# Where buffers live in a two-layer decoder step: normed tokens, partial sums and token-major weights moved to other slots

## The chip, the cores and the metric

The kernel runs on one core of one Trainium2 chip. The metric is the device time of one launch in microseconds (us). The kernel before the change takes 1732.09 us, the median of three runs that lie between 1731.93 and 1732.36 us.

## The reference: what is computed

One inference step of a two-layer decoder runs for a prompt of 512 tokens and for 8 samples of 4 new tokens each. Both groups share the weights, so the kernel treats them as one block of 544 tokens of width 1024. All of it is in float32. Layer 0 has one input projection that feeds a state-space branch and a sliding-window attention, and one output projection. Layer 1 has forgetting attention over a paged cache. Each layer then attends to 256 memory tokens, and ends with a feed-forward part:

```
h = rms_norm(x, norm_ffn[l])
g, u = split(h @ w_ffn_in[l])        # 1024 -> 2 x 2816
x = x + (silu(g) * u) @ w_ffn_out[l]
```

Outputs are the two normed token blocks, the new states and the new cache rows.

## The kernel before, in words

**Operands in two halves.** A float32 product is made of three TensorE products of rounded halves. Whatever TensorE reads, weights and tokens alike, is split first: ScalarE (ACT) writes the rounded high part, VectorE (DVE) subtracts it from the source and writes the low part. `wpiece` (L141) does this for most weights: it loads a piece into `raw` (two buffers), and the halves go to `wh` and `wl` (three buffers each). A buffer taken from such a ring waits until the readers of its last content are done. Names in a profile row are tiles: `xh`, `xl` are halves of the tokens, `fh`, `fl` (and `f1`) those of the feed-forward weights, `ps` is a PSUM bank.

**Slots.** Large activations share 13 slots `H` of 128 x 2176 floats (L119). The two halves of the 544 tokens of a norm take four of these, the hidden values of the feed-forward part `hh` and `hl` one each per four tiles.

**The token-major weights.** In layer 0 the weights `we_v` (L601) multiply with tokens on the output partitions and give V and the state-space time steps; in layer 1 `wd_v` does the same (L973). Each is two pieces of 128 x 1088, loaded by `wpiece`, between the keys (`kT`, L428) and the queries (`we_q`).

**The feed-forward part** (`ffn`, L1469) makes 22 hidden tiles of 128. The first three are plain (`plain`): per tile a gate and a value product for two token chunks, 256 and 288 wide, each followed by L1496 (gate times the norm's scale, DVE), L1497 (silu, ACT), L1498 (times the scale, POOL) and L1499 (value times gate, DVE), and by a split into `hh` and `hl` (L222, L225). The other 19 tiles use seven block products instead of eight: the weight's and the tokens' quarters are combined first. `factors` (L1436) loads a tile's weights (`fr`, two buffers, 1024 KB) and makes the sums s1 to s4 with DVE (L1457 to L1460) and all splits (L1450, L1451). `operands` (L1405) writes the normed tokens `xn`, makes the sums t1 to t4 with POOL (L1424, L1429), and splits them into seven factors `xf` (b11, b21, b22, t1 to t4; L1415 on ACT, L1417 or L1419 on DVE). Both `xn` (two) and `xf` (seven) are slots `H`. `product` (L1467) is 12 matmuls of 128 x 272.

Per tile the order is: `begin` (a11 x b11, copied to the partial sum S0 by L1540), `second` (a12 x b21, plus S0, L1546), `third` (s1 x t1; s2 x t2, copied to S1 by L1553), `fourth` of the tile before (s3 x t3, copied to S2 by L1557, summed to G1 by L1558, silu L1559), `last` (a22 x t4, silu L1564; s4 x b22, plus S1, L1567; gate times value L1569 on POOL; split). S0, S1, S2, G1 and the gate SG are parts of one tile `ft`, beside two value buffers U that alternate between tiles.

**What sets the order.** Each engine runs its instructions in program order. Neither that order nor the addresses stand in the source: a scheduler in the compiler orders the instructions by its own cost estimates, and a packer lays buffers that are not alive together over each other. A change of buffers therefore moves instructions and waits too. Loads are issued by SyncE (SP), also in order.

## Time and profile before

The profiled execution took 1733.22 us by the device clock; the span of its trace is 1731.4 us, so 1.8 us lie outside the span. Its mean granted TensorE clock is 0.983.

| | busy us | share of the span |
|---|---|---|
| PE (matmul) | 1666.6 | 96% |
| PEld (weight load) | 1531.3 | 88% |
| DVE | 1200.5 | 69% |
| ACT | 776.9 | 45% |
| POOL | 429.4 | 25% |

A row of a timeline reads: start in us, duration, engine, line, operation, output<-input, count, and in brackets the time for which the engine stood idle before it and what ended that. In a table of waits the numbers are the total, how many times, and the longest. In a table of stretches an engine's column is its busy time, with the count of its instructions, followed by the granted clock (PEclk, 1.00 is full speed), the share of the DMA engines, and GB/s.

### The profile page before, as it was taken

What the parts mean: (1) busy time and instruction counts of PE and PEld (TensorE: products, weight loads), DVE (VectorE), ACT (ScalarE), POOL (GpSimd) and SP (SyncE); (2) the same over time, 40 slices, a digit from 0 to 9 for tenths busy, and PEclk for the clock granted to TensorE, in tenths of its full rate; (3) what the DMA queues carried; (4) which work ended last, traced back from release to release, by engine and by line L of the source; (5) the groups of instructions that cost most, each with busy time, mean ns of one, the idle gap of its engine ahead of it and who ended that gap; (6) DMA issues with size and microseconds to landing.
All of it is one profiled execution on the core that took longest, in us unless ns stands there. A gap on an engine that the chain in (4) does not pass through costs nothing.

```text
span 1731.4 us, 32174 instructions
## 1 busy us (share of the span) xinstructions
PE 1666.6 (96%) x12824; PEld 1531.3 (88%) x12824; DVE 1200.5 (69%) x2142; ACT 776.9 (45%) x1575; POOL 429.4 (25%) x550
## 2 busy tenths in 40 slices
PE   6999999989999989999999999889999899999997
PEld 6988899866997989999999997556898899999997
DVE  6667679867866897777766567335577887777753
ACT  4345435344545454444435345325446354444443
POOL 5022323566422511111113013012222501111112
PEclk9999999989999999999999999899999999999999
DMA  4211423127533142222214423444442142323212
GB/s 157 90 50 50 131 93 129 44 94 253 182 98 135 62 146 86 97 98 86 98 40 135 149 62 113 159 171 151 166 143 91 65 148 92 107 78 110 86 47 80
DMA packets 57106, 189.24 MB, mean 109 GB/s; under 512 B 6044, under 2 KB 16060, under 8 KB 49084
## 3 DMA queue, kind: packets, MB, share of 16 engines
q1 hardware_dynamic: 55268, 184.83, 31.9%
q8 instruction: 101, 1.65, 0.4%
q10 hardware_dynamic: 1608, 1.83, 0.4%
q0 software_dynamic: 80, 0.52, 0.1%
q14 instruction: 49, 0.40, 0.1%
HBM read 172.22 MB, written 14.95 MB: 108 GB/s over the span
## 4 chain that ended last, share of the span: by engine, by line
PE 84%; DVE 7%; DMA 3%; ACT 2%; issue 1%; POOL 1%; SPq 1%; DVEq 0%; ACTq 0%; POOLq 0%
PE ps L135 59%; PE ps L1467 23%; PE ps L138 3%; DMA kv<-fox_kv 1%; DVE wl L152 1%; DMA raw<-we_x 1%; DVE fl L1451 1%; DVE xn L1409 1%; DVE xl L228 1%; SPq L1158 0%; DMA raw<-wfo 0%; POOL ft L1498 0%; DMA hb<-state 0%; DVE fr L1457 0%; DVE xs L853 0%
## 5 line engine op out<-in xcount | busy, mean ns | idle before, releaser
L1467 PE MATMUL ps<-xf,fh 128*128 128x272 f32 x1824 | 355.3, 291 | 11.4 <-DVE ft L1496 3.7
L135 PE MATMUL ps<-xh,wh 128*128 128x288 f32 (+1 forms) x1088 | 319.3, 295 | 8.8 <-ACT wh L151 7.9
L135 PE MATMUL ps<-xl,wh 128*128 128x288 f32 (+1 forms) x1088 | 319.5, 295 | 1.2 <-DVE xl L228 1.0
L135 PE MATMUL ps<-xh,wl 128*128 128x288 f32 (+1 forms) x1088 | 317.9, 293 | 1.9 <-DVE wl L152 1.9
L1467 PEld LDWEIGHTS ps<-xf,fh 128*128 128x128 f32 x1824 | 290.1, 190 | 13.6 <-ACT xf L1415 6.8
L1467 PE MATMUL ps<-xf,fl 128*128 128x272 f32 x912 | 258.2, 292 | 0.0
L135 PEld LDWEIGHTS ps<-xh,wh 128*128 128x128 f32 x1088 | 206.4, 190 | 12.6 <-ACT wh L151 7.9
L135 PEld LDWEIGHTS ps<-xl,wh 128*128 128x128 f32 x1088 | 206.3, 190 | 7.1 <-issue 4.9
L1569 POOL TENSOR_TENSOR ft<-ft 128x544 f32<-128x544 f32 x38 | 78.9, 2076 | 527.7 <-DVE ft L1567 512.7
L135 PEld LDWEIGHTS ps<-xh,wl 128*128 128x128 f32 x1088 | 206.5, 190 | 3.3 <-DVE wl L152 2.2
L151 ACT CAST wh<-raw 128x1024 fp32r<-128x1024 f32 (+2 forms) x128 | 130.9, 1023 | 173.8 <-PE ps L135 98.8
L1451 DVE TENSOR_TENSOR fl<-fr,fh 128x1024 fp32r<-128x1024 f32 x114 | 173.7, 1525 | 23.8 <-ACT fh L1450 23.6
L152 DVE TENSOR_TENSOR wl<-raw,wh 128x1024 fp32r<-128x1024 f32 (+2 forms) x128 | 160.7, 1256 | 30.4 <-ACT wh L151 15.2
L1467 PEld LDWEIGHTS ps<-xf,fl 128*128 128x128 f32 x912 | 170.8, 190 | 0.0
L1450 ACT CAST fh<-fr 128x1024 fp32r<-128x1024 f32 x114 | 119.8, 1053 | 94.0 <-DVE fr L1458 51.8
L135 PE MATMUL ps<-hl,oh 128*128 128x256 f32 (+1 forms) x512 | 147.4, 289 | 0.0
L135 PE MATMUL ps<-hh,ol 128*128 128x256 f32 (+1 forms) x512 | 147.1, 288 | 0.0
L135 PE MATMUL ps<-hh,oh 128*128 128x256 f32 (+1 forms) x512 | 146.2, 288 | 0.0
L237 POOL TENSOR_TENSOR room<-room,sq 128x256 f32<-128x256 f32 (+1 forms) x96 | 84.9, 886 | 184.7 <-ACT sq L236 182.7
L135 PEld LDWEIGHTS ps<-hl,oh 128*128 128x128 f32 x512 | 96.5, 188 | 0.0
L135 PEld LDWEIGHTS ps<-hh,oh 128*128 128x128 f32 x512 | 96.3, 189 | 0.0
L135 PEld LDWEIGHTS ps<-hh,ol 128*128 128x128 f32 x512 | 96.3, 188 | 0.0
(425 smaller groups left out, 3783.6 us busy)
## 6 DMA issues: line engine op xcount, KB each, us to landing
fr<-wfi SPq DMA_DIRECT2D x38, 1024.0 KB
or<-wfo SPq DMA_DIRECT2D x32, 512.0 KB
kv<-fox_kv SPq DMA_DIRECT2D x64, 256.0 KB
raw<-wo_e SPq DMA_DIRECT2D x16, 512.0 KB
xk<-mem_k SPq DMA_DIRECT2D x8, 1024.0 KB
xv<-mem_v SPq DMA_DIRECT2D x8, 1024.0 KB
raw<-we_x SPq DMA_DIRECT2D x12, 512.0 KB
raw<-wfi SPq DMA_DIRECT2D x12, 512.0 KB
```

The source lines that it names most:

```text
L135: self.nc.tensor.matmul(out, lhsT, rhs, start=start, stop=stop)
L138: self.nc.tensor.transpose(out, in_, self.ident[0:k, 0:k])
L151: nc.scalar.copy(hi[:, 0:n], raw[:, 0:n])
L152: nc.vector.tensor_tensor(lo[:, 0:n], raw[:, 0:n], hi[:, 0:n].bitcast(F32), ALU.subtract)
L228: return nc.vector.scalar_tensor_tensor(ll, src, g, hh.bitcast(F32), ALU.mult, ALU.subtract)
L237: nc.gpsimd.tensor_tensor(acc, acc, sq[:, 0:N], ALU.add)
L1409: nc.vector.scalar_tensor_tensor(xn[k], self.x[k], self.par[:, st["g"] + k:st["g"] + k + 1], st["b"], ALU.mult, ALU.mult)
L1450: nc.scalar.copy(hi, t)
L1451: nc.vector.tensor_tensor(lo, t, hi.bitcast(F32), ALU.subtract)
L1467: self.nc.tensor.matmul(ps, w[a][:, k], x[:, b, k], start=start and k == 0 and i == 0, stop=k == 3 and i == 2, skip_group_check=True)
L1569: nc.gpsimd.tensor_tensor(p["u"], p["u"], SG, ALU.mult)
```

## The change

- `we_v` and `wd_v` no longer use the ring of `wpiece`. The new `vpieces` takes three slots `H` (`vr`, `vh`, `vl`), and puts the two pieces side by side in each. The ring's tiles shrink from 1088 to 1024 columns.
- The normed tokens `xn` of the feed-forward part leave the slots `H` and get two buffers in the pool of that part.
- The partial sums S0, S1, S2 and G1 lose their buffers. S0 and S1 are written to the two halves of the value buffer U and summed in place; S2 and G1 are written into the gate's buffer, of which there are now two (G) that alternate between tiles.
- Two small buffers move: the QS tile loses 64 columns, and `ncs` of the paged attention moves into a tile that exists already.

No arithmetic is added or removed, and each engine has as many instructions as before.

```diff
@@ wpiece
-        raw = self.wp.tile([P, 1088], F32, tag="raw", bufs=2, name=self.nm("raw"))
+        raw = self.wp.tile([P, 1024], F32, tag="raw", bufs=2, name=self.nm("raw"))
...
+    def vpieces(self, src):
+        nc = self.nc
+        raw, hi, lo = self.H("vr"), self.H("vh", F32R), self.H("vl", F32R)
+        out = []
+        for i in range(2):
+            s = slice(1088 * i, 1088 * i + 1088)
+            nc.sync.dma_start(raw[:, s], src[i])
+            nc.scalar.copy(hi[:, s], raw[:, s])
+            nc.vector.tensor_tensor(lo[:, s], raw[:, s], hi[:, s].bitcast(F32), ALU.subtract)
+            out.append([t[:, s].rearrange("p (k w) -> p k w", w=272) for t in (hi, lo)])
+        return out
...
-            wv = [self.wpiece(I["we_v"][i], 4, 272) for i in range(2)]
+            wv = self.vpieces(I["we_v"])
...
-            wv = [self.wpiece(I["wd_v"][i], 4, 272) for i in range(2)]
+            wv = self.vpieces(I["wd_v"])
@@ operands
         xn = Big(self, "xn")
+        xn.h = [fp.tile([P, 4 * NT], F32, tag="xn", bufs=2, name=self.nm("xn")).rearrange("p (k t) -> p k t", k=4) for _ in range(2)]
@@ ffn
-            t = fp.tile([P, 10 * HT], F32, name="ft")
-            part = lambda a, n: t[:, HT * a:HT * (a + n)]
-            U, SG, S0, S1, S2, G1 = (part(0, 2), part(2, 2)), part(4, 2), part(6, 1), part(7, 1), part(8, 1), part(9, 1)
+            t = fp.tile([P, 4 * NT], F32, name="ft")
+            U, G = ([t[:, NT * i:NT * i + NT] for i in r] for r in ((0, 1), (2, 3)))
...
-                    g, s = U[n % 2][:, o:o + N], SG[:, o:o + N]
+                    g, s = U[n % 2][:, o:o + N], G[n % 2][:, o:o + N]
...
-                nc.scalar.copy(S0, R)
-                return {"n": n, "w": w, "R": R, "u": U[n % 2]}
+                nc.scalar.copy(U[n % 2][:, 0:HT], R)
+                return {"n": n, "w": w, "R": R, "u": U[n % 2], "g": G[n % 2]}
...
-                nc.vector.tensor_tensor(p["u"][:, 0:HT], R3, S0, ALU.add)
+                nc.vector.tensor_tensor(p["u"][:, 0:HT], R3, p["u"][:, 0:HT], ALU.add)
...
-                nc.scalar.copy(S1, p["R"])
+                nc.scalar.copy(p["u"][:, HT:NT], p["R"])
...
-                nc.scalar.copy(S2, p["R"])
-                nc.vector.tensor_tensor(G1, p["R2"], S2, ALU.add)
-                nc.scalar.activation(SG[:, HT:NT], G1, AF.Silu, scale=-1.0)
+                g = p["g"][:, HT:NT]
+                nc.scalar.copy(g, p["R"])
+                nc.vector.tensor_tensor(g, p["R2"], g, ALU.add)
+                nc.scalar.activation(g, g, AF.Silu, scale=-1.0)
...
-                nc.scalar.activation(SG[:, 0:HT], p["R"], AF.Silu, scale=-1.0)
+                nc.scalar.activation(p["g"][:, 0:HT], p["R"], AF.Silu, scale=-1.0)
...
-                self.last = nc.vector.tensor_tensor(p["u"][:, HT:NT], p["R2"], S1, ALU.add)
+                self.last = nc.vector.tensor_tensor(p["u"][:, HT:NT], p["R2"], p["u"][:, HT:NT], ALU.add)
```

The change moves lines as well: after it, the lines from L145 to L163 read the same up to L152, and those of the feed-forward part are 13 to 15 higher (L1415 becomes L1430, L1419 L1434, L1451 L1466, L1467 L1482, L1496 L1510, L1553 L1567). Tile numbers are 3 to 6 lower.

What the compiler makes of it, at three places:

DVE in layer 0, around the keys. `wl_40`, `wl_43` (after: `vl_40`) are low halves of `we_v`, the other `wl` those of the first `we_q` pieces; L279 (after: L292) copies the scale that the keys need. Before:

```order
L152 TENSOR_TENSOR wl_40_319<-raw_38_316,wh_39_318 128x1088
L271 TENSOR_SCALAR col_2_79<-ps_22_161 128x2
L152 TENSOR_TENSOR wl_43_325<-raw_41_322,wh_42_324 128x1088
L279 COPY room_70<-ps_23_166 128x256
L152 TENSOR_TENSOR wl_57_508<-raw_55_505,wh_56_507 128x1024
L428 TENSOR_TENSOR kT_206<-ps_34_212,room_70 128x256
L428 TENSOR_TENSOR kT_206<-ps_36_264,room_70 128x256
```

and in the changed kernel:

```order
L165 TENSOR_TENSOR vl_40_318<-vr_38_316,vh_39_317 128x1088
L284 TENSOR_SCALAR col_2_79<-ps_22_161 128x2
L165 TENSOR_TENSOR vl_40_318<-vr_38_316,vh_39_317 128x1088
L152 TENSOR_TENSOR wl_54_505<-raw_52_502,wh_53_504 128x1024
L152 TENSOR_TENSOR wl_60_564<-raw_58_561,wh_59_563 128x1024
L292 COPY room_70<-ps_23_166 128x256
L441 TENSOR_TENSOR kT_206<-ps_34_212,room_70 128x256
L441 TENSOR_TENSOR kT_206<-ps_36_264,room_70 128x256
```

Two `we_q` splits now stand ahead of the scale's copy, and none between it and `kT`. The loads of the two pieces wait for the two `we_k` splits, where they waited for the two `we_v` splits.

DVE in layer 0, where the seven-product part begins. `fl` are low halves of the weight sums, `xf` with L1419 or L1417 (after: L1434, L1432) those of t1 to t4 in this order. Before:

```order
L1460 TENSOR_TENSOR fr_1082_7165<-fr_1082_7165 128x512
L1451 TENSOR_TENSOR fl_1087_7177<-fr_1082_7165,fh_1086_7176 128x1024
L1451 TENSOR_TENSOR fl_1089_7182<-fr_1082_7165,fh_1088_7181 128x1024
L1496 TENSOR_TENSOR ft_6755<-ps_1080_7109,room_70 128x288
L1499 TENSOR_TENSOR ft_6755<-ps_1079_7054,ft_6755 128x256
L1419 TENSOR_TENSOR xf_1068_7027<-xn_1063_7006,xf_1068_7027 128x1088
L1417 SCALAR_TENSOR_TENSOR xf_1069_7031<-xn_1063_7006,xf_1069_7031 128x1088
L225 TENSOR_TENSOR hl_1042_6757<-ft_6755,hh_1041_6756 128x256
L1499 TENSOR_TENSOR ft_6755<-ps_1081_7110,ft_6755 128x288
L1419 TENSOR_TENSOR xf_1070_7034<-xn_1064_7011,xf_1070_7034 128x1088
L1419 TENSOR_TENSOR xf_1071_7038<-xn_1064_7011,xf_1071_7038 128x1088
```

and in the changed kernel:

```order
L1475 TENSOR_TENSOR fr_1079_7162<-fr_1079_7162 128x512
L1434 TENSOR_TENSOR xf_1065_7024<-xn_1060_7003,xf_1065_7024 128x1088
L1466 TENSOR_TENSOR fl_1084_7174<-fr_1079_7162,fh_1083_7173 128x1024
L1466 TENSOR_TENSOR fl_1086_7179<-fr_1079_7162,fh_1085_7178 128x1024
L1510 TENSOR_TENSOR ft_6752<-ps_1077_7106,room_70 128x288
L1432 SCALAR_TENSOR_TENSOR xf_1066_7028<-xn_1060_7003,xf_1066_7028 128x1088
L1513 TENSOR_TENSOR ft_6752<-ps_1076_7051,ft_6752 128x256
L1434 TENSOR_TENSOR xf_1067_7031<-xn_1061_7004,xf_1067_7031 128x1088
L1434 TENSOR_TENSOR xf_1068_7035<-xn_1061_7004,xf_1068_7035 128x1088
L238 TENSOR_TENSOR hl_1039_6754<-ft_6752,hh_1038_6753 128x256
L1513 TENSOR_TENSOR ft_6752<-ps_1078_7107,ft_6752 128x288
```

t1 moves ahead of both weight splits, t3 and t4 ahead of a value split. On ACT the high half of t1 moves ahead of both weight casts. The packer lays the next tile's weights (`fr_1090`) over `xn_1060`, so the load of these waits for t2 (`xf_1066`); before, it waited for `fl_1089`, the second weight split.

PE at the same place. After the 24 matmuls of s1 x t1 and s2 x t2, the program before went on with s3 x t3 (`xf_1070`, 12 matmuls), and then to four matmuls of the next tile (`fh_1094`). In the changed kernel the next tile's four (`fh_1091`) come first:

```order
L1482 MATMUL ps_1087_7182<-xf_1066_7028,fl_1084_7174 128x272
L1482 MATMUL ps_1098_7256<-xf_1062_7013,fh_1091_7238 128x272 x2
L1482 MATMUL ps_1099_7285<-xf_1063_7016,fh_1091_7238 128x272 x2
L1482 MATMUL ps_1087_7182<-xf_1067_7031,fh_1085_7178 128x272 x2
L1482 MATMUL ps_1087_7182<-xf_1067_7031,fl_1086_7179 128x272
```

On ACT the cast that gives `fh_1091` likewise moves ahead of the copy of S1 (L1567), on which s3 x t3 waits, because both use one PSUM bank. The order in layer 1 is the same. Elsewhere the scheduler also reorders the end of layer 0's mixing part (state-space output and the `wo_e` weights) and the last group of the paged attention (cache loads ahead of `wo_d` loads).

23 lines of the change are left out of this document (12 added, 11 removed).

## The prediction, made before the changed kernel was run

> **What bounds the kernel now.** I read the page's busy times first, then the table of PE's waits:
>
> ```profile
> PE 1666.6 (96%) x12824; PEld 1531.3 (88%) x12824; DVE 1200.5 (69%) x2142; ACT 776.9 (45%) x1575; POOL 429.4 (25%) x550
> ```
>
> ```profile
> PE ps L1467 <- DVE ft L1496: 3.7, 1, 3.7
> PE ps L1467 <- DVE xf L1419: 3.0, 2, 2.2
> PE ps L1467 <- ACT xf L1415: 2.6, 1, 2.6
> PE ps L1467 <- ACT ft L1553: 2.0, 4, 0.5
> PE ps L135 <- DVE kT L428: 1.8, 1, 1.8
> ```
>
> TensorE bounds the whole; the change touches no matmul, so it can move only PE's waits, the 64.8 us of the span in which PE is not busy. The waits quoted are those at its places: 10.3 us in the two starts of the seven-product part (3.7 + 3.0 + 2.6, and two of the four waits of 0.5) and 1.8 us at the keys. What a wait there costs besides is in the clock:
>
> ```profile
> 604.00:626.00 22.00, 16.74 (x107) 15.86 (x106) 20.36 (x24) 13.08 (x21) 5.32 (x3) 0.84 0.45 168
> 1364.00:1392.00 28.00, 22.92 (x162) 22.01 (x161) 27.07 (x25) 12.41 (x19) 14.72 (x7) 0.88 0.32 122
> 1000.00:1030.00 30.00, 29.09 (x235) 28.25 (x233) 21.22 (x46) 14.73 (x32) 2.86 (x8) 1.00 0.24 71
> ```
>
> The first two stretches are the starts, in layers 0 and 1; the third is undisturbed. In the starts DVE is busy 20.36 of 22 and 27.07 of 28 us: there DVE, not PE, is what lasts.
>
> **The keys (layer 0).** The chain of waits, then DVE:
>
> ```profile
> 24.56 4.14 DMA raw<-we_q
> 29.86 1.22 DVE wl L152
> ```
>
> ```profile
> 8.94 1.63 DVE L152 TENSOR_TENSOR wl<-raw,wh 128x1024 fp32r<-128x1024 f32 x1
> 23.26 1.28 DVE L152 TENSOR_TENSOR wl<-raw,wh 128x1088 fp32r<-128x1088 f32 x1
> 28.03 0.42 DVE L279 COPY room<-ps 128x256 f32<-128x256 f32 x1 [2.22 <-PE ps L135]
> 31.57 0.36 PE L135 MATMUL ps<-wh,xh 128*128 128x272 f32 x1 [1.79 <-DVE kT L428]
> ```
>
> The first `we_q` load leaves at 24.56, when the first `we_v` split frees its buffer; its split (29.86 to 31.08) is in front of `kT` on DVE. In the change the load waits for the first `we_k` split instead, which ends at 8.94 + 1.63 = 10.57, so the data are there some ten us earlier. Two splits of 1.22 us then fall into DVE's idle 2.22 us before the copy at 28.03, and overrun it by 0.2 us. `kT` follows the copy, at about 28.7 instead of 31.0, and PE's next work, which is ready at 31.57 - 1.79 = 29.78, need not wait: **-1.8 us**, bounds -1.8 and -1.0 (casts late by 0.8). No later wait of PE hangs on a load that this leaves where it was, so I let the gain reach the end. `wd_v` in layer 1 has the same cure but no wait of PE in the list: 0.
>
> **The start of the seven-product part, layer 0.** DVE, ACT, SP and PE of before:
>
> ```profile
> 608.55 0.68 DVE L1460 TENSOR_TENSOR fr<-fr 128x512 f32<-128x512 f32 x1
> 609.41 2.89 DVE L1451 TENSOR_TENSOR fl<-fr,fh 128x1024 fp32r<-128x1024 f32 x2 [0.19 <-ACT fh L1450]
> 612.23 0.45 DVE L1496 TENSOR_TENSOR ft<-ps,room 128x288 f32<-128x288 f32 x1
> 612.93 1.28 DVE L1419 TENSOR_TENSOR xf<-xn,xf 128x1088 fp32r<-128x1088 f32 x1
> 614.13 1.89 DVE L1417 SCALAR_TENSOR_TENSOR xf<-xn,xf 128x1088 fp32r<-128x1088 f32 x1
> 616.64 2.48 DVE L1419 TENSOR_TENSOR xf<-xn,xf 128x1088 fp32r<-128x1088 f32 x2
> ```
>
> ```profile
> 616.75 0.43 ACT L222 CAST hh<-ft 128x288 fp32r<-128x288 f32 x1 [1.02 <-DVE ft L1499]
> 619.82 0.39 ACT L1553 COPY ft<-ps 128x272 f32<-128x272 f32 x1 [2.64 <-PE ps L1467]
> 620.10 1.05 ACT L1450 CAST fh<-fr 128x1024 fp32r<-128x1024 f32 x1
> 621.05 0.62 ACT L1450 CAST f<-fr 128x512 fp32r<-128x512 f32 x1
> ```
>
> ```profile
> 612.33 0.33 SPq L1440 DMA_DIRECT2D fr<-wfi  x1
> ```
>
> ```profile
> 611.69 0.39 PE L1467 MATMUL ps<-xf,fh 128*128 128x272 f32 x1 [2.61 <-ACT xf L1415]
> 614.26 0.59 PE L1467 MATMUL ps<-xf,fh 128*128 128x272 f32 x1 [2.17 <-DVE xf L1419]
> 619.41 0.38 PE L1467 MATMUL ps<-xf,fl 128*128 128x272 f32 x1
> 620.26 0.52 PE L1467 MATMUL ps<-xf,fh 128*128 128x272 f32 x2 [0.47 <-ACT ft L1553]
> 622.51 1.78 PE L1467 MATMUL ps<-xf,f 128*128 128x272 f32 x12
> ```
>
> From 614.26 to 619.41 lie 22 matmuls, 0.23 us each; 12 from 620.26 to 621.87 take 0.13 each. So after 5 us of waiting PE is at about half rate for 5 us, 2.2 us lost beside the waits. The mark to hold on to: at 622.5 PE has done 40 matmuls (s1 x t1, s2 x t2, s3 x t3, four of the next tile).
>
> Now the new order with these durations. Until the last weight sum (L1460 ends 609.23) nothing moves. DVE then: t1 to 610.4 (1.2); the two weight splits to 613.1 (2.7); gate 613.5 (0.4); t2 to 614.8 or 615.4 (1.3 to 1.9); value 615.2; t3 and t4 to about 618. PE has t1 and the first split at 611.9 and does s1 x t1 until 613.2 to 614.2. s2 x t2 needs the copy of S0, which on ACT stands behind the gate's silu (after 613.5) and a value's high half (after 615.2): 616.0. It runs 616.0 to 618.7 at 0.23. So t1 and t2 are no longer late, and PE is ahead by 0.7 us here. But next come four matmuls of the next tile. Its load leaves after t2 at 614.8 instead of 612.33. How long it takes is in the DMA rates of that place, slices of 0.75 us from 600:
>
> ```profile
> GB/s 0 0 0 0 0 0 0 22 0 0 0 0 0 0 0 0 0 120 55 360 415 442 393 426 464 393 431 388 344 273 339 49 0 0 0 0 0 0 0 0
> ```
>
> The rate rises at 612.75, and 1024 KB are through by 616.5: 4.2 us from issue. So now 619.0; the cast stands behind a value's high half (L1499 ends 618.9, cast 0.43): 619.4 to 620.4. Then the four matmuls; the copy of S1 waits behind this cast and the next (0.62): 621.4; s3 x t3 runs from there, 12 matmuls, to 622.9 at 0.13 or 624.1 at 0.23. The 40 are done at 622.9 to 624.1 instead of 622.5: +0.4 to +1.6, **+1.0 us**. The earlier operands gain nothing, since the load that xn now holds up, and the queue behind it on ACT, take the place of the old wait. What follows (next tile's low half, 1.2 us after its cast; a22 x t4) is ready in time.
>
> The Trainium skill ("TensorE: Matmul & The Clock Gate", Part 1: The HAM clock gate) says that the clock halves after an idle window of about 3.4 us, and is released after about as long of work. Before, the trace agrees (4.8 us of waits, then half rate for 5 us). By that rule the new order, whose longest single wait here is 2.8 us, would stay at full clock, and the lower end, +0.4, would hold.
>
> **Layer 1** has the same order, another time:
>
> ```profile
> 1381.78 0.45 DVE L1496 TENSOR_TENSOR ft<-ps,room 128x288 f32<-128x288 f32 x1
> 1382.37 0.57 PE L1467 MATMUL ps<-xf,fh 128*128 128x272 f32 x1 [3.73 <-DVE ft L1496]
> 1383.81 0.59 PE L1467 MATMUL ps<-xf,fh 128*128 128x272 f32 x1 [0.87 <-DVE xf L1419]
> 1389.12 0.52 PE L1467 MATMUL ps<-xf,fh 128*128 128x272 f32 x2 [0.47 <-ACT ft L1553]
> ```
>
> Here s1 x t1 waits for the gate (L1496), since it needs that PSUM bank. t1 (1.3 us) moves ahead of it, so it ends 1.0 to 1.3 us later, at 1383.2; s1 x t1 runs to 1386.0, and the copy of S0 (behind a value) comes at 1386.2. s2 x t2 ends at 1388.1. The next tile's load leaves after t2 (1.9 us as in layer 0), at 1385.0, lands at 1389.2, is cast at 1390.3; S1 is copied at 1391.3, and s3 x t3 ends at 1392.8. Before, the 40 were done at 1389.12 + 2.2 (the same stretch as 620.26 to 622.51) = 1391.4: **+1.4 us**, from 0 to +3.
>
> **Partial sums in place.** In the steady tiles the copy of S0 now waits for the value buffer, so for the low half of the hidden values two tiles earlier:
>
> ```profile
> 666.57 0.71 DVE L225 TENSOR_TENSOR hl<-ft,hh 128x544 fp32r<-128x544 f32 x1
> 669.41 0.39 ACT L1540 COPY ft<-ps 128x272 f32<-128x272 f32 x1
> ```
>
> That split ends 2.1 us before the copy starts: 0. The third and fourth of the 0.5 us waits for S1 stand at the end of each layer, in an order that stays: 0.
>
> **The two other reordered places.**
>
> ```profile
> 410.00:458.00 48.00, 47.52 (x325) 42.68 (x324) 38.89 (x73) 23.25 (x45) 25.51 (x23) 0.96 0.66 228
> 1147.00:1222.00 75.00, 65.48 (x550) 40.56 (x549) 35.70 (x104) 33.94 (x96) 11.65 (x19) 0.98 0.58 203
> ```
>
> At the end of layer 0's mixing PE idles 0.5 us and loses 0.04 x 48 = 1.9 us of clock, so at most 2.4 us can be won; as much can be lost where work that filled a wait moves. I take 0, bounds -2.4 and +2.4. In the paged attention 9.5 us are idle, and the weights that come later (issued after the cache's loads) are used tens of matmuls later; fill work moves from one wait to another: 0, bounds -2 and +2.
>
> **The sum.** -1.8 + 1.0 + 1.4 = +0.6 us, on the profiled 1733.22 (1731.4 span and 1.8 around it), which is 1.1 above the median. Against the median: 1732.09 + 0.6 = **1732.7 us**.
>
> **Rivals.**
> - *The starts do gain.* For it: 10.3 us of waits there and 2.2 + 1.6 us of half clock (in layer 1, 22 matmuls from 1383.81 to 1388.4, 0.07 to 0.08 more than 0.13 each), 14.1 in all, and two of the operands really come earlier. Against it: DVE is full, and t4, whose end closes the DVE work, moves by 1 us only. If the next tile's load lands in 2 us less and the clock stays up, half of the 14.1 goes: -7.0 - 1.8 = -8.8, **1723.3**.
> - *The next tile's load becomes the bound.* Mechanism: issued after t2 and used ahead of s3 x t3, each us by which it lands later than 4.2 us after issue is a us of PE in both layers. Five loads are issued in that stretch; it decides from 5 us on. With 2.5 us more per layer: +0.6 + 5.0, **1737.7**. Against it: it is the first of the five.
> - *The sums in place bind*: if the low half is over 2.1 us later than now, each further 0.2 us costs 38 x 0.2 = 7.6 us: **1740.3**. Nothing in those tiles delays it.
> - *The early weights do not come early* (other loads in front, DVE's splits late): the 1.8 us stay, **1734.5**; that is inside "no change".
>
> **How the numbers follow.** A measurement of this kernel can tell about 0.2%, 3.5 us, from no change: 1728.6 to 1735.6. My forecast with its bounds (and the fourth rival) 55%, the gain 22%, the late load 20%, the sums 3%. Of the forecast's own range, 1729 to 1736.5, a little passes 1735.6; some of the late load's stays below it. So faster 0.23, same 0.54, slower 0.23. For 8 in 10 the range reaches halfway to the two larger rivals: 1727 to 1738.
>
> **What would show it.** Right: PE's wait at `kT` gone; in both starts the load `fr` issued behind L1432, PE waiting on the `fh` cast (L1465) where it waited for `xf`, the 40 matmuls done within 2 us of the old mark. Wrong: no wait for that cast and a clock of 1.00 in the starts (the gain); new waits of S0's copy in the steady tiles; the mixing's or the paged attention's stretch longer or shorter by over 2.5 us, which would make the sum one of places that I set to 0.

## The result, and the profile after

The changed kernel takes 1743.63 us (median of four runs, 1742.01 to 1744.77), beside 1732.01 us for the kernel before in the same comparison. The ratio is 1.0068 with a 95% interval of 1.0051 to 1.0085: 0.7% slower, outside the forecast's range. The profiled execution took 1743.81 us; its span is 1742.0, 10.6 us longer than before.

The page's busy times of the changed kernel, then PE's waits (total, times, longest):

```profile
PE 1670.2 (96%) x12824; PEld 1536.1 (88%) x12824; DVE 1198.0 (69%) x2142; ACT 767.9 (44%) x1575; POOL 432.8 (25%) x550
```

```profile
PE ps L1482 <- ACT fh L1465: 4.8, 3, 2.3
PE ps L1482 <- ACT xf L1430: 4.7, 1, 4.7
...
PE ps L138 <- DMA lg<-fox_logf,pg: 2.4, 1, 2.4
PE ps L135 <- DVE CmYi L964: 1.9, 1, 1.9
...
PE ps L1482 <- ACT ft L1554: 1.5, 1, 1.5
PE ps L1482 <- DVE fl L1466: 1.3, 1, 1.3
...
PE ps L135 <- POOL room L412: 1.2, 1, 1.2
```

The wait for `kT` is gone, and of the 3.0 us for t1 to t4 by DVE 0.6 us are left. In their place stand the cast of the next tile's weights (L1465), a wait for `xf` by ACT, a wait for a gather (`lg`), one for `CmYi` (state-space output), and one for POOL at the keys. PE is also 3.6 us longer busy with the same 12824 matmuls: part of the loss is clock.

**Where the time went.** Every kernel here has 12824 matmuls, so I cut each trace at the starts of the same matmuls by number, at places where the program orders agree. Each stage is the time between two such starts. The difference to the stage of before, in us (one profiled execution each):

| stage (matmul numbers; length before) | forecast | measured |
|---|---|---|
| start with keys (0 to 210; 37.7) | -1.8 | -1.15 |
| end of layer 0's mixing (2690 to 3200; 92.2) | 0 | **+5.75** |
| seven-product start, layer 0 (4130 to 4530; 59.7) | +1.0 | +2.26 |
| layer 1's first part with the gather (7200 to 7400; 27.4) | 0 | **+5.30** |
| paged attention (7700 to 9000; 200.3) | 0 | -3.08 |
| seven-product start, layer 1 (10100 to 10600; 71.1) | +1.4 | +2.57 |
| the six other stages together | 0 | -0.7 |

The sum of the measured column is +10.9; work behind the last of these starts gives 0.3 back. Two places that the forecast set to 0 make as much as the whole result.

### The profile page after: what moved, and what is told of

It reads as the page before. It is cut to its first block, busy times and chain, and to the rows that moved or that the text cites. A ratio compares the mean times of both kernels' runs of the same rounds, so it can differ in the third digit from the quotient of the medians.

```text
span 1742.0 us, 32009 instructions
## 1 busy us (share of the span) xinstructions
PE 1670.2 (96%) x12824; PEld 1536.1 (88%) x12824; DVE 1198.0 (69%) x2142; ACT 767.9 (44%) x1575; POOL 432.8 (25%) x550
## 4 chain that ended last, share of the span: by engine, by line
PE 83%; DVE 6%; DMA 5%; POOL 2%; issue 2%; ACT 2%; SPq 1%; DVEq 0%; POOLq 0%; ACTq 0%
PE ps L135 58%; PE ps L1482 23%; PE ps L138 3%; DMA kv<-fox_kv 1%; DMA raw<-we_x 1%; DVE fl L1466 1%; POOL room L412 1%; DVE xn L1424 1%; SPq L1172 1%; DMA fr<-wfi 1%; DVE xs L866 1%; DMA lg<-fox_logf,pg 1%; DVE wl L152 0%; DVE xl L241 0%; POOL ft L1512 0%
## 5 line engine op out<-in xcount | busy, mean ns | idle before, releaser
L1482 PE MATMUL ps<-xf,fh 128*128 128x272 f32 x1824 | 356.8, 292 | 12.6 <-ACT fh L1465 4.8
L1482 PEld LDWEIGHTS ps<-xf,fh 128*128 128x128 f32 x1824 | 291.5, 191 | 15.1 <-ACT fh L1465 5.6
L1482 PE MATMUL ps<-xf,fl 128*128 128x272 f32 x912 | 259.7, 293 | 1.3 <-DVE fl L1466 1.3
L151 ACT CAST wh<-raw 128x1024 fp32r<-128x1024 f32 (+1 forms) x124 | 126.0, 1019 | 137.3 <-PE ps L135 92.3
L1466 DVE TENSOR_TENSOR fl<-fr,fh 128x1024 fp32r<-128x1024 f32 x114 | 172.5, 1515 | 14.1 <-ACT fh L1465 14.1
L1482 PEld LDWEIGHTS ps<-xf,fl 128*128 128x128 f32 x912 | 172.0, 191 | 1.5 <-DVE fl L1466 1.5
L152 DVE TENSOR_TENSOR wl<-raw,wh 128x1024 fp32r<-128x1024 f32 (+1 forms) x124 | 156.1, 1261 | 19.6 <-PE ps L135 9.5
L1465 ACT CAST fh<-fr 128x1024 fp32r<-128x1024 f32 x114 | 119.7, 1050 | 45.3 <-DVE fr L1473 39.0
```

Source lines behind the costliest of these rows:

```text
L151: nc.scalar.copy(hi[:, 0:n], raw[:, 0:n])
L152: nc.vector.tensor_tensor(lo[:, 0:n], raw[:, 0:n], hi[:, 0:n].bitcast(F32), ALU.subtract)
L1465: nc.scalar.copy(hi, t)
L1466: nc.vector.tensor_tensor(lo, t, hi.bitcast(F32), ALU.subtract)
L1482: self.nc.tensor.matmul(ps, w[a][:, k], x[:, b, k], start=start and k == 0 and i == 0, stop=k == 3 and i == 2, skip_group_check=True)
```

## The experiments

No kernel leaves work out; `held_query_load` and no other adds a store (32 bytes). `self.after(a, b)` only tells the scheduler to put `a` behind `b` in the order; it adds no wait. Diffs stand against the changed kernel. The experiments' medians are compared with the kernel before on the same chip, where its medians lay between 1730.8 and 1732.1 us and single runs between 1726.0 and 1737.3. One execution of it can so lie some 5 us beside the median, and single executions of the experiments lie up to 10 us beside theirs. The stages are those of one execution of each kernel, which need not be a typical one: the profiled one took 1747.6 us of `samples_behind` (the slowest of six, median 1740.8) and 1737.1 of `early_memory_split` (the fastest of ten, median 1741.3). For all runs, the stages of the table above (differences to before), the median and the ratio with its interval:

| kernel | start | end of mixing | FFN start L0 | gather | paged | FFN start L1 | median us | ratio |
|---|---|---|---|---|---|---|---|---|
| the change | -1.2 | 5.8 | 2.3 | 5.3 | -3.1 | 2.6 | 1743.6 | 1.0068 [1.0051, 1.0085] |
| in_place_only | 0.0 | 1.0 | -1.0 | 0.0 | -1.2 | 0.2 | 1732.6 | 1.0000 [0.9990, 1.0010] |
| no_vpieces | -1.7 | 0.0 | 2.1 | 0.0 | -3.7 | 2.8 | 1735.8 | 1.0024 [1.0011, 1.0037] |
| no_xn | -0.6 | 8.0 | -1.1 | 6.4 | 0.2 | -0.2 | 1748.6 | 1.0100 [1.0081, 1.0120] |
| half_xn | 1.9 | 5.7 | -0.7 | 6.4 | -3.5 | -0.4 | 1744.7 | 1.0067 [1.0049, 1.0086] |
| half_xn_old_ring | -0.4 | 0.5 | -0.3 | 0.0 | 3.6 | -0.7 | 1737.0 | 1.0030 [1.0018, 1.0041] |
| early_page_list | -1.1 | 5.4 | 2.1 | 0.0 | 1.4 | 1.3 | 1743.3 | 1.0072 [1.0050, 1.0095] |
| held_query_load | 1.7 | 5.7 | 1.8 | 0.0 | -0.9 | 3.1 | 1743.4 | 1.0070 [1.0051, 1.0088] |
| early_memory_split | -2.1 | 3.9 | 2.3 | 1.4 | -2.6 | 2.4 | 1741.3 | 1.0048 [1.0028, 1.0069] |
| samples_behind | 1.9 | 3.6 | 2.3 | 4.1 | -4.6 | 3.0 | 1740.8 | 1.0050 [1.0030, 1.0071] |
| split_behind | 0.4 | 4.8 | 2.2 | 1.2 | -4.9 | 2.8 | 1739.7 | 1.0054 [1.0033, 1.0074] |
| split_and_samples | -0.6 | 6.6 | 2.4 | 6.5 | -5.9 | 2.4 | 1743.1 | 1.0065 [1.0046, 1.0085] |
| old_order_there | 0.3 | 0.1 | 2.6 | 0.7 | -2.8 | 2.4 | 1735.8 | 1.0028 [1.0011, 1.0045] |
| three_mended | 1.7 | 6.3 | -0.7 | 0.0 | -5.5 | -0.1 | 1733.6 | 1.0018 [0.9999, 1.0038] |
| mended_again | -0.6 | 3.4 | -0.2 | 0.0 | -4.5 | 0.4 | 1733.8 | 1.0007 [0.9991, 1.0023] |
| all_mended | 0.4 | 3.4 | -0.3 | 0.9 | -6.6 | -0.6 | 1732.1 | 1.0010 [0.9993, 1.0026] |
| all_mended_2 | 0.4 | -0.2 | 0.2 | 2.4 | 4.3 | -0.7 | 1740.4 | 1.0056 [1.0037, 1.0076] |
| mended_old_paged | -0.6 | -1.2 | -1.3 | 2.6 | -4.5 | 0.5 | 1728.6 | 0.9993 [0.9979, 1.0007] |
| mended_third_order | 0.4 | 1.6 | -0.3 | 0.3 | -8.3 | -0.1 | 1726.4 | 0.9965 [0.9951, 0.9978] |

### One part at a time

`in_place_only` keeps the sums in place and undoes the rest (the old ring, old slots of `xn`, QS and `ncs`).

```diff
-            wv = self.vpieces(I["we_v"])
+            wv = [self.wpiece(I["we_v"][i], 4, 272) for i in range(2)]
-            wv = self.vpieces(I["wd_v"])
+            wv = [self.wpiece(I["wd_v"][i], 4, 272) for i in range(2)]
...
-        xn.h = [fp.tile([P, 4 * NT], F32, tag="xn", bufs=2, ...) for _ in range(2)]
```

> The kernel before with the partial sums in place, nothing else moved. Theory (the sums in place cost nothing, since the value buffer comes free 2.1 us before S0's copy): 1732.0 us, within 0.2% of before, and the 19 steady tiles of both layers as long as before. Rival (the sums wait for the low half of the hidden values): a wait of S0's copy in each tile, 0.2 us x 38 = 7.6 us, 1739.6 us.

1732.55 us, ratio 1.0000; the 2170 matmuls of layer 0's steady tiles take 0.01 us more. The sums in place cost nothing, as forecast.

`no_vpieces` takes the first two pairs of lines of that diff (and the wider ring), `no_xn` its last line.

> The changed kernel with the token-major weights back in the ring of 1088 columns; normed tokens in their own buffers and sums in place stay. Theory (three separate losses, in the changed kernel's trace +5.6 us at the end of layer 0's mixing and +5.3 us at the start of layer 1, both from the weights' slots, +2.4 us in each start of the seven-product part, from the normed tokens' buffers): only the two starts lose, 1732.0 + 4.8 = 1736.8 us; with the 3 us that the paged attention gained, if these belong to the normed tokens, 1733.8 us. No wait of TensorE for the gather of fox_logf. Rival (the losses outside the starts come from the packer's whole layout, whichever buffer is moved): +5 us or more at the end of the mixing or at the start of layer 1 here too, 1740 us or more.

> The changed kernel with the normed tokens back in the slots H; weights in half-tensor slots and sums in place stay. Theory: both starts of the seven-product part as before (no wait for the fh cast of the next tile), the end of the mixing +5.6, the start of layer 1 +5.3, the keys -1.2: 1732.0 + 9.7 = 1741.7 us; 1738.7 us if the paged attention's 3 us go with the weights. Rival (the starts are late because DVE's order changed everywhere): starts +2 us each here too, 1743.6 us.

Without `vpieces` the end of the mixing and the gather are as before (0.0 and 0.0), while the two starts keep their loss (2.1, 2.8). Without the buffers of `xn` it is the other way round (8.0 and 6.4; -1.1 and -0.2). So each loss goes with one edit: the two large ones with the token-major weights, the two starts with `xn`. `no_xn` is the slowest kernel of all although it undoes a part that costs: with another packing the end of the mixing and the gather came out worse still, by 3.4 us together, and the paged attention 3.3 us longer.

### The seven-product starts: what the load of the next tile waits for

The chain that ended last in the changed kernel, in layer 0 (start, us, what), and then PE there:

```profile
613.87 1.20 DVE xf L1434
615.07 2.81 DVE fl L1466 x2
617.88 0.37 DVE ft L1510
618.25 1.21 DVE xf L1432
...
619.59 4.99 DMA fr<-wfi
...
624.66 1.05 ACT fh L1465
...
625.76 0.78 PE ps L1482 x4
```

```profile
614.13 0.39 PE L1482 MATMUL ps<-xf,fh 128*128 128x272 f32 x1 [0.40 <-ACT fh L1465]
615.13 0.39 PE L1482 MATMUL ps<-xf,fh 128*128 128x272 f32 x1 [0.61 <-DVE xf L1434]
616.80 0.39 PE L1482 MATMUL ps<-xf,fl 128*128 128x272 f32 x1 [1.28 <-DVE fl L1466]
...
620.56 0.82 PE L1482 MATMUL ps<-xf,fh 128*128 128x272 f32 x2 [1.49 <-ACT ft L1554]
...
625.76 1.33 PE L1482 MATMUL ps<-xf,fh 128*128 128x272 f32 x6 [2.11 <-ACT fh L1465]
...
629.62 0.66 PE L1482 MATMUL ps<-xf,fh 128*128 128x272 f32 x2
...
631.45 0.42 PE L1482 MATMUL ps<-xf,fh 128*128 128x272 f32 x2
```

t1 and the splits are earlier, t2 follows, and the load leaves behind t2, as forecast: all times here are 4.7 us later than in before, so 619.59 is the forecast 614.8 within 0.1. It lands after 4.99 us, estimated 4.2 (an estimate from the DMA rates). In layer 1 the same chain reads

```profile
1391.66 1.21 DVE xf L1432
...
1392.93 4.84 DMA fr<-wfi
...
1397.79 1.05 ACT fh L1465
```

To test whether the loss comes from that load's wait, `half_xn` puts one half of `xn` back into a slot `H`. The packer then lays the next tile's weights elsewhere, and their load waits for the second weight split (L1466) again, while t1 still stands ahead of the weight splits.

```diff
-        xn.h = [fp.tile([P, 4 * NT], F32, tag="xn", bufs=2, ...) for _ in range(2)]
+        xn.h = [self.H("xn").rearrange(...), fp.tile([P, 4 * NT], F32, tag="xn", bufs=1, ...)]
```

> The changed kernel with the first half of the normed tokens back in a slot H and only the second half in a buffer of its own, so that the packer lays the next tile's weights elsewhere and their load no longer waits for t2; t1 still stands ahead of the weight splits on DVE. Theory (the load behind t2 is what costs 2.4 us per start): that loss is gone in both layers, and t1, which comes early, may win 1 to 2 us per start: 1743.6 - 4.8 = 1738.8 us, down to 1735. Rival (the loss is DVE's new order): 1743.6 us, with TensorE waiting in the starts for splits and not for the load.

The starts fall from +2.3 and +2.6 to -0.7 and -0.4. So t1 ahead of the weight splits is not what costs. What costs goes with the load behind t2, but not with its lateness alone: in `half_xn` the scheduler also puts S1's copy (L1567) ahead of the next tile's cast on ACT, and s3 x t3 ahead of the next tile's four matmuls on PE, as in the kernel before. The late load and the order behind it come and go together here, and no run separates them. The earlier t1 alone wins nothing that shows: `no_xn` has -1.1 and -0.2, and `in_place_only`, which runs the old order, -1.0 and +0.2. That -1.0 is clock. The old order's two waits of 2.6 and 2.2 us are there, but the stretch that had a clock of 0.84 in the execution of before has 0.92 here:

```profile
604.00:626.00 22.00, 16.75 (x114) 15.91 (x113) 21.20 (x24) 12.71 (x20) 6.66 (x4) 0.92 0.44 168
```

The kernel's time does not fall (1744.7), since `half_xn` keeps the two losses of `vpieces`, and its own start and the stretch after it (up to matmul 2690) came out 6.8 us longer than before. In one matmul stretch of layer 0 (numbers 1000 to 2600) PE waits for `PTn` for 2.2 us in this trace, 1.1 in that of the change, and the clock halves after it.

### The gather in layer 1

The entries of the tile `lg` of the changed kernel between 930 and 1020 us; the same gather (L1103) in the kernel before; SP's issues of the changed kernel and of before:

```profile
L138 PE MATMUL ps<-room,lg x16: 311/311/366, 999.7 to 1002.0; 64*128 64x64 f32 x16
L1118 POOL DMA_INDIRECT lg<-fox_logf,pg x1: 1134/1134/1134, 990.6 to 990.6; - x1
...
DMA to landing us min/median/max: 8.9/8.9/8.9
```

```profile
L138 PE MATMUL ps<-room,lg x16: 221/222/272, 990.7 to 992.1; 64*128 64x64 f32 x16
L1103 POOL DMA_INDIRECT lg<-fox_logf,pg x1: 1134/1134/1134, 984.0 to 984.0; - x1
...
DMA to landing us min/median/max: 6.2/6.2/6.2
```

```profile
988.14 1.77 SPq L145 DMA_DIRECT2D raw<-wd_q  x2
```

```profile
981.78 0.71 SPq L145 DMA_DIRECT2D raw<-wd_q  x1
...
991.07 0.34 SPq L145 DMA_DIRECT2D raw<-wd_q  x1
```

The gather fetches the cached gates by a list of pages. It is issued 6.6 us later than before, which is just the lateness of everything at that place (the stages ahead of it add up to 6.6). But it needs 8.9 us instead of 6.2, and before, it landed only half a us ahead of its use (984.0 + 6.2 = 990.2, used at 990.7). What is new beside it is one load. Before, the next query weights (512 KB) left at 981.78, ahead of the gather, and at 991.07, when it had landed. Now two loads leave ahead of it, from 988.14 to 989.91, because `wd_v` no longer holds buffers of the ring. This is the very effect that the forecast counted as a gain at the keys. PE waits 2.44 us, then its clock halves (311 instead of 222 ns per small matmul).

Two runs separate "too many loads beside it" from "issued too late":

```diff
 # early_page_list: the list of pages is loaded without a place in the order
-        self.after(nc.scalar.dma_start(pg, I["page_col"]), last)
+        nc.scalar.dma_start(pg, I["page_col"])
...
 # held_query_load: the sixth query piece's load follows a 32-byte store that needs the gather
+        self.lgout = nc.sync.dma_start(scr, lg[0:1, 0:8])
...
+                    self.after(self.wlast, self.lgout)
```

> The changed kernel, but the 64 page numbers of the gather are loaded at the program's start and not just ahead of it, so that the gather waits only for GpSimd and not 3.4 us for that load. Theory (the gather's landing is what TensorE waits for at 997 us, and the wait also costs the clock behind it): the wait of 2.4 us and the half clock behind it go, the stretch from matmul 7200 to 7400, 5.3 us longer than before, comes back to within 0.5 us of before: 1743.6 - 5.3 = 1738.3 us. Rival (the matmuls of that stretch run slow for another reason, their own weights or the clock): no change, 1743.6 us.

> The changed kernel, but the sixth load of wd_q (512 KB, issued at 989 us, one us ahead of the gather) waits until the gather has landed, by a store of 32 bytes of the gathered rows that stands ahead of it on SyncE. Theory (the gather lands in 8.9 us instead of 6.2 us because one more load of wd_q moves beside it): it lands in 6.2 to 7 us, TensorE's wait of 2.4 us shrinks to 0 to 0.6 us, the stretch from matmul 7200 to 7400 wins 2.4 to 5 us: 1739 to 1741 us. Rival (the gather is slow because of the 1 MB stored and loaded just before it, or for a reason of its own): 8.5 us or more to landing, 1743.6 us or more.

Both end the loss (0.02 and -0.01 us), and they do it differently. In `early_page_list` the gather still takes 8.4 us beside the loads, but is issued some 3 us earlier against PE's work. In `held_query_load` it is not earlier, and its landing falls below that of before as soon as the second load is away:

```profile
L138 PE MATMUL ps<-room,lg x16: 221/223/273, 999.8 to 1001.3; 64*128 64x64 f32 x16
...
DMA to landing us min/median/max: 5.7/5.7/5.7
```

Over all twenty traces, by the query loads that are issued from 3 us before to 3 us after the gather: with one load it lands after 5.7 to 6.4 us (five traces), with two after 7.0 to 9.9 (seven), with four after 8.4 to 10.4 (eight). The loads beside the gather are the cause of its late landing. Neither kernel is faster as a whole than the change (1743.3 and 1743.4). In the profiled executions the paged attention (+1.4 and -0.9 instead of -3.1) and the start took the gain. The 5.3 us are also not the loss of every execution: in the six traces with two loads beside a gather as late as that of the change, this stage loses 0.7 to 6.5 us, 3.2 in the mean. That the medians do not fall by even that is not explained; the intervals, 3 to 4 us to both sides in each kernel, leave room for it.

### The end of layer 0's mixing

Three waits of PE (timeline), then the stretch around the first (columns: PE, PEld, DVE, ACT and POOL busy; the clock is the third number from the end):

```profile
417.89 0.41 PE L135 MATMUL ps<-room,CmYi 128*128 128x32 f32 x2 [1.85 <-DVE CmYi L964]
440.83 0.39 PE L135 MATMUL ps<-xh,wl 128*128 128x256 f32 x1 [1.35 <-DVE wl L152]
445.61 0.39 PE L135 MATMUL ps<-xh,wh 128*128 128x256 f32 x1 [1.22 <-ACT wh L151]
```

```profile
410.00:458.00 48.00, 43.59 (x274) 37.56 (x273) 37.24 (x69) 19.91 (x39) 22.86 (x21) 0.89 0.59 212
417.00:421.00 4.00, 3.11 (x26) 2.69 (x26) 3.91 (x9) 1.04 (x1) 4.00 (x4) 0.79 0.57 190
421.00:425.00 4.00, 4.00 (x22) 3.11 (x21) 0.75 (x2) 0.51 (x1) 0.82 (x2) 0.50 0.36 142
425.00:429.00 4.00, 4.00 (x11) 3.13 (x11) 3.83 (x15) 1.70 (x4) 0.00 (x0) 0.50 0.31 126
```

The same stretch of before has 325 matmuls and a clock of 0.96; this has 274 and 0.89. Three waits of 4.4 us and 5.3 us of clock (0.11 x 48), less the 0.5 and 1.9 us that before loses there, are 7.3 us. From matmul 2900 on, just ahead of these waits, to 3200 the kernel is 6.8 us longer; up to 2900 the stage was 1.0 us shorter, which gives the 5.75. By the clock records 10.2 us from 419.3 on are at half clock. The wait is not all of that: in the kernel before the same small matmuls (`CmYi`, `sE`) follow each other without a wait, and 3.4 us at half clock stand behind them. Moved there are the splits of the cross-attention's weights (`mkv`, `wl`) against the state-space output on DVE, and the matmuls that use them on PE. No line there is edited; the slots of `vpieces` change which buffers overlap, and the scheduler then takes another order. I took the moved pieces one at a time:

```diff
 # early_memory_split: the update of the state-space output behind a split of the memory's value weights
+                self.after(u, self.mvlo)
...
 # samples_behind: the samples' matmuls behind the third piece of the memory's values
+            self.after(self.lastmm, self.mv2)
...
 # split_behind: the third piece's split behind the copy of the memory's scale
+                self.after(self.wlo, self.mbcopy)
...
 # split_and_samples: the last two together
```

> The changed kernel with one scheduling hint: the low half of the fourth piece of the memory's value weights is made on VectorE ahead of the state-space output's sample updates (L972), as in the kernel before, and not behind them. Theory (this split, held by updates that wait for TensorE, frees its load buffer 8 us late, and all loads of wo_e behind it are late): the waits of TensorE at 439 and 444 us go, and of the 6.9 us that the stretch from matmul 2970 to 3200 has become longer 4 to 6 go: 1738 to 1739.6 us. Rival (the loss comes from TensorE's own new order at that place, or from the clock after the wait at 416 us): 1743.6 us, within 1 us.

> The changed kernel with a hint on TensorE's order: the 24 small matmuls of the samples' state-space output (CmYi, sxdt) stand behind the third piece of the memory's values, as in the kernel before, and not ahead of all four. Theory, formed anew (the loss at the end of the mixing is TensorE's 1.85 us wait for CmYi at 416 us, with no work put ahead of it, and the half clock of some 10 us that follows; the late wo_e loads are a consequence): no wait for CmYi, clock 1.00 through that stretch, 4.5 to 6.5 us won, 1737 to 1739 us. Rival (the late splits on VectorE set the end of that stretch whatever TensorE does): 1741 us or more.

> The changed kernel with one hint on VectorE's order: the low half of the third piece of the memory's value weights (wl of raw<-wxv) stands behind the copy of the memory's scale (L292) and behind CmYi, as that copy does in the kernel before, and not ahead of both. Theory, formed for the third time (this split waits 0.9 us for its cast and takes 1.3 to 1.6 us, with the two drains that TensorE waits for queued behind it; the half clock after that wait does the rest): CmYi is ready 2.4 us earlier, TensorE's 1.85 us wait for it goes, the clock stays up, and 4 to 6 us of the stretch from matmul 2900 to 3200 come back: 1737.6 to 1739.6 us. Rival (the samples' matmuls standing ahead of the memory's values is what costs, since the work behind them comes late in any case): 1742 us or more.

> The changed kernel with that hint and the one of the earlier run together, so that TensorE and VectorE both stand in that stretch as in the kernel before. Theory: neither the wait of 1.85 us for CmYi nor that of 3.05 us for the scale's copy (L292), both queued behind the same split; the whole 5 to 6.7 us of the stretch come back: 1737 to 1738.6 us. Rival (the loss lies after this place, in the late loads of wo_e): 1741 us or more.

By these traces they won 1.8, 2.2, 0.9 and -0.9 of the 5.75 us. Each removes or shifts a wait and gets another: `early_memory_split` keeps 1.87 us at `CmYi` and has new ones of 0.88 and 1.12 for `mkv`; `samples_behind` waits 3.04 us for the scale's copy (L292) instead of 1.85 for `CmYi`; `split_behind` has no wait for `CmYi`, but 2.15 and 0.65 for the weights behind it; `split_and_samples` waits 1.18 us for the scale's copy and 2.17 for `hb`. No single piece is "the" cause. So I put back nearly all of the old order there at once, with the new slots left in the source as they are:

```diff
 # old_order_there: samples_behind, and
+            if l == 0 and kp == 0:
+                self.after(self.wlo, self.mrs)
+            if l == 0 and kp == 2:
+                self.after(self.wlo, self.mklast)
+                self.kp2 = self.wlo
...
+            self.after(nc.vector.tensor_tensor(Yi[...], ...), self.kp2)
```

> The changed kernel with hints that put VectorE and TensorE at the end of the mixing into the order of the kernel before, almost row for row (first piece's split behind L284, third piece's split behind the four products with the memory's scale, CmYi behind that split, the samples' matmuls behind the third piece). Theory (the loss there is the order alone: one late drain of VectorE is enough for a wait and a half clock, which is why hints one by one only moved it): no wait over 0.6 us between matmul 2800 and 3200 but those of before, 5 to 7 us of 6.8 won, 1736.6 to 1738.6 us. Rival (the loss is not the order but where the slots lie, or when the loads land): 1742 us or more.

```profile
410.00:458.00 48.00, 48.00 (x323) 43.66 (x322) 38.71 (x71) 22.87 (x44) 25.34 (x23) 0.93 0.65 223
...
421.00:425.00 4.00, 4.00 (x19) 3.32 (x18) 3.69 (x4) 1.39 (x2) 3.00 (x3) 1.00 0.78 278
```

The stage is +0.08 us, PE has no wait at all in that stretch, and the kernel takes 1735.78. Of the stage's 114 DVE rows of before all but 2 stand there in the old order, of the 510 on PE all but 42. The loads come back with it: those of `wo_e`, of which four leave 10 to 16 us later in the change (from the stage's start), leave within 0.3 us of before. So with the new slots the order makes the 5.75 us. How much of that is the order itself and how much the loads that it holds up, no run separates.

### All mends together, and what is left

The mends combined: `three_mended` is `half_xn`, `early_page_list` and `early_memory_split`; `mended_again` is the first two with `samples_behind`; `all_mended` adds `split_behind` to that; `half_xn_old_ring` is `half_xn` with `we_v` and `wd_v` back in the old ring; `all_mended_2` is `half_xn`, `early_page_list` and `old_order_there`.

```diff
 # three_mended, mended_again, all_mended, all_mended_2
-        self.after(nc.scalar.dma_start(pg, I["page_col"]), last)
+        nc.scalar.dma_start(pg, I["page_col"])
...
+        xn.h = [self.H("xn").rearrange(...), fp.tile([P, 4 * NT], F32, tag="xn", bufs=1, ...)]
...
 # half_xn_old_ring
+            wv = [self.wpiece(I["we_v"][i], 4, 272) for i in range(2)]
```

> The changed kernel with three edits together: the first half of the normed tokens in a slot H, the page numbers loaded early, the memory's split ahead of the updates. Theory (the losses are these three places and they add): 1743.6 - 5.3 - 5 - 5.5 (starts) = 1728 us, between 1726 and 1732, so at or a little below the kernel before, by what the keys (0.5 to 1) and the paged attention (up to 3) win. Rival (taking one wait away uncovers the next in the same stretch): 1735 us or more.

> The changed kernel with the first half of the normed tokens in a slot H, the page numbers loaded early, and the samples' matmuls behind the memory's values. Theory: three losses of 4.9, 5.3 and about 6 us go, 1743.6 - 16.2 = 1727.4 us, between 1725 and 1730, which is below the kernel before by the keys and the paged attention. Rival (the paged attention's 3 us are chance and the keys win under 1 us): 1730 to 1732 us, no difference from before.

> The kernel before with the sums in place and only the second half of the normed tokens in a buffer of its own; the token-major weights stay in the ring of 1088 columns. Theory: no loss at the end of the mixing, at the start of layer 1 or in the two starts; the paged attention, whose order the normed tokens' move changes, wins 0 to 3 us: 1729 to 1732 us. Rival (the paged attention's gain needs both moves): 1732 us.

> The changed kernel with the first half of the normed tokens in a slot H, the page numbers loaded early, and both hints at the end of the mixing. Theory: against the earlier run without the split's hint (1733.75 us) the 5 us that the stretch from matmul 2900 to 3200 still lost are gone: 1728.5 to 1730 us, against 1731.7 us of the kernel before: no difference that can be told, or faster by up to 0.2%. Rival (a further wait appears there): 1733 us or more.

> The changed kernel with the first half of the normed tokens in a slot H, the page numbers loaded early, and that whole old order at the end of the mixing. Theory: 5 us below the earlier run with two hints (1732.1 us): 1726 to 1728 us, against 1731.7 us of the kernel before: faster by 0.2 to 0.3%, from the paged attention. Rival (no gain beyond the losses mended): 1731 to 1733 us.

The first, second and fourth come back to no measurable change (1.0018, 1.0007, 1.0010), with the end of the mixing still at +6.3, +3.4 and +3.4. `half_xn_old_ring` has all four places within 0.7 us of before and is still slower (1.0030), as is `all_mended_2` (1.0056), in which the order at the end of the mixing is whole. What they have in common is the paged attention: +3.6 and +4.3 us, beside -4.5 to -6.6 in the other three. No mend touches it.

Several orders of it occur among the kernels. They differ on PE, ACT and DVE (where the samples' and the prompt's softmax and products stand among each other) and by one or a few weight loads on SP; POOL's is the same in the kernels shown below. Two further kernels, made from `all_mended_2` with one hint less and then one other more, both in layer 0, got two other orders there in layer 1:

```diff
 # mended_old_paged: all_mended_2 without
-            if l == 0 and kp == 0:
-                self.after(self.wlo, self.mrs)
 # mended_third_order: that, and the last matmul of the memory's fourth keys product behind the scale's broadcast
+                if l == 0 and n == 3 and k == KD - 1:
+                    self.after(self.lastmm, self.mpb)
```

> The kernel of the run before (three places mended, 1740.4 us) without the hint on the first piece's split, by which the scheduler gives the paged attention the order that it had in the earlier run with two hints (1732.1 us). Theory (the 8.6 us between those two kernels are the order of the paged attention, 140.7 against 130.0 us from matmul 8100 to 9000, and nothing at the end of the mixing): that stretch takes 130 to 133 us again, the end of the mixing at most 2 us more than before, 1728 to 1730 us. Rival (the paged attention's length is chance from run to run, whatever its order): 133 to 140 us there, 1733 us or more.

> The same kernel with one more hint, on TensorE (the fourth keys product of the memory behind the scale's broadcast), by which the paged attention gets the order of the run with two hints alone (split_and_samples, 130.9 us). Theory: 131 to 133 us from matmul 8100 to 9000, the end of the mixing within 1.5 us of before, 1727.5 to 1730 us. Rival (chance): 133 to 140 us there, 1733 us or more.

The paged attention as one stretch, in `all_mended_2`, `mended_old_paged` and `mended_third_order`, in that order:

```profile
1037.30:1241.90 204.60, 183.25 (x1303) 125.59 (x1302) 103.21 (x276) 89.20 (x246) 36.68 (x66) 0.94 0.44 154
```

```profile
1034.00:1229.90 195.90, 180.77 (x1303) 125.05 (x1302) 102.94 (x276) 89.11 (x246) 36.83 (x66) 0.95 0.47 158
```

```profile
1039.80:1231.80 192.00, 179.38 (x1303) 124.35 (x1302) 103.00 (x276) 88.89 (x246) 36.78 (x66) 0.96 0.47 160
```

The same 1303 matmuls last 204.6, 195.9 and 192.0 us; the first kernel waits 8.8 us for cache loads (`kv`), the others 3.3 and 5.5. The medians follow: 1740.4, 1728.6 and 1726.4. Not all of the stretches' difference is the order: `all_mended` has the same order there as `mended_old_paged` and takes 193.7 us. `mended_third_order` beats both kernels: 0.9965 of before [0.9951, 0.9978], 4.4 us by the medians on its chip. It is not what the change itself moves that wins there. Its starts and its keys are at -0.3, -0.1 and +0.4 us, and the one stage that is much shorter in its trace is the paged attention (-8.3), in an order that the change had not asked for. Whether the old kernel with that order would be as fast was not tried, nor which of the moved instructions makes it.

The -3.1 us that the change itself shows in the paged attention is not a gain to count on either: `early_page_list` and `held_query_load` have the same order there, and +1.4 and -0.9 us.

## Why the prediction was wrong, point by point

**The two places set to 0** are the steps that failed. In this execution they make 11.05 us, as much as the whole loss. The step on the end of the mixing said "at most 2.4 us can be won; as much can be lost where work that filled a wait moves. I take 0, bounds -2.4 and +2.4". The upper bound was borrowed from the gain and has nothing to do with a loss: a new order can put any wait there, and behind the 1.85 us of wait and the small matmuls after it the half clock lasts 10.2 us. Measured +5.75, which `old_order_there` takes away by the order. The row for an upper bound was in the same profile: the clock loss of the seven-product starts.

The step on layer 1 said "`wd_v` in layer 1 has the same cure but no wait of PE in the list: 0". It asked whether an early load could remove a wait, and not what the early loads collide with. The gather's landing (6.2 us, half a us ahead of its use) could be read in the trace of before. Measured +5.30: 2.44 of wait, the rest clock; that the late gather makes it is shown twice, by the earlier list and by the held load. The prediction's own sign of being wrong, a mixing or paged stretch off by over 2.5 us, came true.

**The seven-product starts**: mechanism right, size off. The load behind t2, the cast of the next tile's weights and s3 x t3 behind it came as worked out. The term that was too small is the clock. In layer 0 PE is at the mark of 40 matmuls 1.4 us later than before (forecast 0.4 to 1.6), counted like the stages, but then runs at half rate from 627.5 to 631, where the old order had recovered, and loses another 0.9. In layer 1 it is 2.7 us late at the mark (forecast 1.4, bounds 0 and 3): s3 x t3 begins within 0.2 us of the forecast, but its 12 matmuls last 2.6 us where the step took 1.5. The landing, 4.99 and 4.84 us where the step took 4.2, moved less: 0.5 us at the cast in layer 0, and nothing in layer 1, where the load left 0.6 us earlier than worked out. The rival "the next tile's load becomes the bound" counted from a landing of 5 us on; the landing stayed just below that, and the loss lies between the forecast and that rival (1.0 + 2.5 and 1.4 + 2.5). "The starts do gain" falls: `half_xn` has the early t1 without the late load and wins nothing that shows over the old order.

The rows above show the clock falling without a long wait: 0.40, 0.61 and 1.28 us with single matmuls between them, and it is at half rate from 617.3 to 624.1 (in such a stretch a pair lasts 0.66 us, as at 629.62, instead of 0.42 at 631.45). The Trainium skill ("TensorE: Matmul & The Clock Gate", Part 1: The HAM clock gate) gives one idle window of about 3.4 us as the condition. By that rule as I used it, on single waits, the start would have stayed at full clock; the trace does not agree, and at the gather one wait of 2.44 us between busy stretches was enough. What the traces do show is a count of idle time in stretches of 3.41 us (last section): in the one from 613.85 to 617.26 PE has no matmul for 64% of the time, all of it in these three waits.

**The keys**: -1.15 in this trace where -1.8 was forecast, and no gain that holds: over the sixteen kernels with `vpieces` the start runs from -2.1 to +1.9, with a mean of +0.1, and `no_vpieces`, which has the old ring, has -1.7. Most of that spread is clock: with no stretch of 3.41 us at half clock between 20 and 42 us the start is at -2.1 and -1.7, with one (as in the kernel before) at -1.2 to +0.4, with two at +0.4 to +1.9. The `kT` wait did go. What took its place stands on POOL, before and after, and on DVE after:

```profile
24.68 1.69 POOL L272 TENSOR_TENSOR col<-col,room 128x2 f32<-128x2 f32 x1 [2.24 <-DVE col L271]
26.35 2.54 POOL L399 TENSOR_TENSOR room<-room,sq 128x288 f32<-128x288 f32 x3
```

```profile
24.65 3.96 POOL L285 TENSOR_TENSOR col<-col,room 128x2 f32<-128x2 f32 x1 [2.24 <-DVE col L284]
28.59 2.53 POOL L412 TENSOR_TENSOR room<-room,sq 128x288 f32<-128x288 f32 x3
```

```profile
24.50 1.28 DVE L165 TENSOR_TENSOR vl<-vr,vh 128x1088 fp32r<-128x1088 f32 x1
25.69 2.35 DVE L152 TENSOR_TENSOR wl<-raw,wh 128x1024 fp32r<-128x1024 f32 x2
29.55 0.42 DVE L292 COPY room<-ps 128x256 f32<-128x256 f32 x1 [1.50 <-PE ps L135]
```

A POOL operation on 128 x 2 values lasts 3.96 us instead of 1.69: it starts beside the first of three splits on DVE (24.50 to 25.78) and ends just behind the last (28.6, after 28.04). What follows on POOL, and with it the copy of the scale (29.55, forecast about 28.2), is late, and PE waits 1.2 us at `room`. The step that failed is "Two splits of 1.22 us then fall into DVE's idle 2.22 us": that time was idle for DVE, and POOL worked in it. Five kernels with `vpieces` (`no_xn` is one) have it the other way round: this operation lasts 1.69 us, but the two `we_q` splits 2.96 us instead of 2.35 and POOL's L412 behind it 3.85 instead of 2.53, and PE waits 1.8 us for that. The Trainium skill ("SBUF — State Buffer", Who interferes with whom) says that a DVE instruction with two inputs in SBUF and a GpSimd instruction that reads SBUF shut each other out; the trace agrees, since the splits are such instructions.

**The sums in place** and the steady tiles: 0 forecast, 0 measured (0.01 us in layer 0 and -0.1 in layer 1, in `in_place_only`). **The paged attention**: 0 forecast with 2 us to both sides; one order spreads from -3.1 to +1.4 between the traces of three kernels, and other orders reach from -8.3 to +4.3. The bounds were too narrow, the value was fair.

## What to carry to other kernels

A buffer that is freed earlier lets a load leave earlier. Ask what that load meets (a gather with half a us to spare, a POOL operation beside the split it feeds) before counting the wait that it removes. Where a scheduler decides the order, a moved buffer reorders places that nobody edited, and such a place is not bounded by its idle time now: cut both traces at the same matmuls, find the stages that moved, and price a new wait with the half clock that follows it.
